# The first loads of a decoder-layer kernel: per-channel vectors ahead on ScalarE's DMA queue, the first 128 channels in two token halves, the other loads in SyncE's queue

## The chip, the cores and the metric

One core of one Trainium2 chip. The metric is the device time of one execution in microseconds (us). Lower is better.

## The reference, cut to what matters

One layer of a decoder trunk on 512 tokens with 1024 channels, all in float32:

```
h  = rmsnorm(x, g_mix)                       # gain g_mix per channel, factor r per token
z  = h @ w_in                                # w_in is 1024 x 9728
A  = retention(z...)                         # 4 heads
Bt = dilated window attention(z...)          # 3 groups of 4 heads, q and k normed and rotated
x  = x + (sig(g_A) * (A @ w_ret_out) + sig(g_B) * (Bt @ w_att_out)) @ w_o
x  = x + relu(rmsnorm(x, g_mlp) @ w_up)^2 @ w_down
x  = x + sig(rmsnorm(x, g_ple) @ w_ple_gate) * (p @ w_ple_proj)
```

The change is at the very beginning: the loading of x and of the first columns of w_in, and the first product h @ w_in, for the queries of attention group 0. There x is multiplied by g_mix alone; the token factor r is put in later.

## The kernel before, in words

**Split products.** Every float32 operand is split into a high part that TensorE takes in its float32r form and the low rest. A product is three matmuls of 128 x 128 by 128 x 512: high by high (L243), high by low (L244), low by high (L245). ScalarE makes the high parts (for weights `whi`, L231; for x `hh`, L452), VectorE the low ones (`wlo`, L232; `hl`, L453).

**First loads (`setup`, L383).** x arrives transposed, as 8 blocks of 128 channels by 512 tokens (`xr`, 256 KB each, L393); the weights of the first product arrive as 8 blocks of 128 rows by 512 columns (`raw`, 256 KB each, L395). All go out on SyncE's queue (SP), x block and weight block in turn, but for two: the first weight block and `gcol` go out on ScalarE's queue (ACT), in that order. `gcol` (128 x 40, 20 KB, L397) holds the per-channel vectors, g_mix in its first 8 columns. Behind these come, all on SP, the rotation table (L431), gains (L435), the four x tiles of 128 tokens (512 KB each, L404) and the next weights (L194). Seven matmuls on zeros (L414) keep TensorE busy meanwhile.

**The first product (`first_panel`, L444).** For each channel block k, ScalarE writes `hh` = x times gain (L452) and VectorE `hl` = x times gain minus `hh` (L453), each in one instruction over 512 tokens. The weight block is split at L231 and L232; for block 0 alone VectorE makes `whi` with a copy (L227) instead. TensorE takes block 0 in a written order: high by high for token tiles 0 to 3 (L471), then `hl` by `whi` for the four (L473), then `hh` by `wlo` (L475). Blocks 1 to 3 follow for the four token tiles, then blocks 4 to 7 tile by tile. Each finished tile is handed to `consume` (L590): four squares with sums on ScalarE (L595), then a rotation on VectorE (L548 to L553). Ahead of the first of these, ScalarE takes the squares of the four x tiles (`token_squares`, L515, L521), whose sums are used for r.

**Order.** In this stretch ScalarE and VectorE take their instructions in the order in which they are written (`manual_schedule`, `keep_in_program_order`); TensorE's order is the scheduler's. The second product (keys) begins where the first ends; its weights are split at L231 and L232 within the queue of the rotations: the first two units behind token tile 1, the others behind tile 3 and the next tables (L577). It uses the same four accumulators, each free when its rotation has read it.

Of the kernel before, what the change touches and what calls it, by code (L numbers as in the profile page):

```python
# [13 lines left out]
AF = mybir.ActivationFunctionType  # L14
ALU = mybir.AluOpType
AX = mybir.AxisListType

P = 128
S = 512
# [52 lines left out]
def R(ap):  # L72
    return ap.bitcast(F32R)


class Block:
# [306 lines left out]
    def setup(self):  # L383
        nc, a = self.nc, self.a
        self.gcol = self.const.tile([P, 40], F32, name="gcol")
        xr = [self.big("xr") for _ in range(2)]
        self.x_cols = [xr[k // 4][:, k % 4] for k in range(KD)]
        for u in range(KD // 2):
            src, _ = self.plan[u]
            raw = self.wraw.tile([P, 1024], F32, tag="raw", name=self.nm("raw")).rearrange("p (k n) -> p k n", k=2)  # L390
            for k in range(2):
                c = slice((2 * u + k) * P, (2 * u + k + 1) * P)
                nc.sync.dma_start(self.x_cols[2 * u + k], a["x_cols"][c])  # L393
                queue = nc.sync if u or k else nc.scalar
                queue.dma_start(raw[:, k], src[k * P : (k + 1) * P])  # L395
                if queue is nc.scalar:
                    nc.scalar.dma_start(self.gcol, a["vec_cols"])  # L397
            self.raws.append((raw, None))
        self.load_tables()
        self.x_tiles = []  # L400
        xb = [self.big("x") for _ in range(2)]
        for t in range(NT):
            v = xb[t // 2].rearrange("p (t c) n -> p t (c n)", t=2)[:, t % 2]
            nc.sync.dma_start(v, a["x"][0, t * P : (t + 1) * P])  # L404
            self.x_tiles.append(v)
        self.fetch(6)
        self.ident = self.const.tile([P, P], F32, name="ident")
        make_identity(nc, self.ident)
        warm = self.tmp("warm")
        nc.vector.memset(warm, 0.0)  # L410
        nc.scalar.activation(warm[:, 500:501], warm[:, 501:502], AF.Copy)
        wb, wps = warm.bitcast(mybir.dt.bfloat16), self.bank("warm")
        for _ in range(WARM):
            nc.tensor.matmul(wps, wb[:, :P], wb[:, :512], start=True, stop=True)  # L414
        self.mhalf = self.const.tile([P, H], F32, name="mhalf")
        nc.gpsimd.memset(self.mhalf, -0.5)
# [27 lines left out]
    def first_panel(self, consume, tables):  # L444
        nc = self.nc
        self.hT = self.new_act(2, "h")
        us = []

        def split_x(k):
            g = self.gcol[:, k : k + 1]  # L450
            h, l = (part[k // 4][:, k % 4] for part in self.hT)
            self.pin(nc.scalar.activation(R(h), self.x_cols[k], AF.Copy, scale=g))  # L452
            nc.vector.scalar_tensor_tensor(R(l), self.x_cols[k], g, h, op0=ALU.mult, op1=ALU.subtract)  # L453

        self.pinned = True
        for u in range(KD // 2):
            self.hook = lambda i: split_x(2 * u + i)
            us += self.units(1)
        self.hook = None
        self.pinned = False  # L460
        banks = [self.gbank() for _ in range(NT)]

        def part(t, k):
            wh, wl = us[k // 2]
            sh, sl = self.stat(self.hT, k, t, False)
            self.mm3(banks[t], sh, sl, wh[:, k % 2], wl[:, k % 2], k == 0, k == KD - 1)

        (wh, wl), mm = us[0], nc.tensor.matmul
        parts = [self.stat(self.hT, 0, t, False) for t in range(NT)]
        for t, (sh, _) in enumerate(parts):  # L470
            mm(banks[t], sh, wh[:, 0], start=True, stop=False)  # L471
        for t, (_, sl) in enumerate(parts):
            mm(banks[t], sl, wh[:, 0], start=False, stop=False)  # L473
        for t, (sh, _) in enumerate(parts):
            mm(banks[t], sh, wl[:, 0], start=False, stop=False)  # L475
        for k in range(1, KD // 2):
            for t in range(NT):
                part(t, k)
        tables()
        self.token_squares()  # L480
        for t in range(NT):
            for k in range(KD // 2, KD):
                part(t, k)
            consume(t, banks[t])
            if t == 1:
                self.pinned = True
                self.ahead(2)
                self.pinned = False
            self.tick()
# [83 lines left out]
    def tables(self, g, n):  # L573
        C = self.tabp.tile([P, NT, HD], F32, tag="tab", name=self.nm("C"))
        Sn = self.tabp.tile([P, NT, HD], F32, tag="tab", name=self.nm("S"))
        for o, part, gi in ((C, 0, 2 * n), (Sn, 1, 2 * n + 1)):
            ins = self.nc.vector.tensor_tensor(  # L577
                o, self.rc[:, 0, :, part * HD : (part + 1) * HD],
                self.gains[:, g, gi].unsqueeze(1).to_broadcast([P, NT, HD]), op=ALU.mult)
            if g == 0:  # L580
                self.tc.keep_in_program_order(ins)
        return C, Sn
# [615 lines left out]
```

## Time and profile before

| | |
|---|---|
| median of 3 runs | 1002.8 us (1002.75 to 1003.02) |
| the profiled execution's own time | 1002.82 us |
| its span in the profile | 1001.1 us |
| TensorE (PE) busy | 991.2 us, 99% of the span |
| VectorE (DVE) busy | 639.5 us, 64% |
| ScalarE (ACT) busy | 445.3 us, 44% |
| first real matmul starts | 6.38 us into the span |

The profiled execution took 1.7 us more than its span. PE's matmuls are pipelined, so that the step between two starts says more than the time of one. PEld is TensorE's weight load. SPq and ACTq are the sequencers of SyncE and ScalarE, where DMAs are issued. An arrow, "<-", names what ended the idle time.

### The profile page before, as it was taken

Reading aid. Unit: us, or ns where it says so; the run is one execution under the profiler, and the core shown is the slowest. Engines: PE = TensorE matmul, PEld = TensorE weight load, DVE = VectorE, ACT = ScalarE, POOL = GpSimd, SP = SyncE. Lnnn points to the kernel's source line nnn. Section 1 sums busy time; section 2 is a strip of 40 time slices with the busy share of each in tenths; the row PEclk is TensorE's granted clock in tenths of the full one; section 3 lists DMA queues with packets and bytes.
Section 4 is the critical chain, followed back from the end, with each engine's and each line's share of the span. In section 5 each row is a group of like instructions: output and inputs, shape, how many; then the busy total and the mean of one; then the engine's idle time right before and its main releaser. Section 6 shows DMA issues by size and latency. Waiting matters only on the chain.

```text
span 1001.1 us, 12319 instructions
## 1 busy us (share of the span) xinstructions
PE 991.2 (99%) x4604; PEld 827.9 (83%) x4604; DVE 639.5 (64%) x931; ACT 445.3 (44%) x844; POOL 98.1 (10%) x98
## 2 busy tenths in 40 slices
PE   8999999999999999999999999999999999999998
PEld 6888899889887888888888877888888888888886
DVE  5967675764779345554643698568468558656953
ACT  6435344433534325342422445654454356355451
POOL 0210220220000010001002010101101001010000
PEclk9999999999999999999999999999999999999999
DMA  9622122323254412222446486849749856784911
GB/s 349 240 84 77 53 84 84 105 86 105 71 159 121 123 43 84 85 82 87 134 142 165 128 211 189 209 110 235 196 112 214 229 146 161 218 183 115 310 54 53
DMA packets 89756, 141.14 MB, mean 141 GB/s; under 512 B 6320, under 2 KB 38368, under 8 KB 89696
## 3 DMA queue, kind: packets, MB, share of 16 engines
q1 hardware_dynamic: 78528, 119.09, 36.7%
q0 software_dynamic: 10880, 20.97, 12.5%
q8 instruction: 36, 0.59, 0.2%
q10 hardware_dynamic: 288, 0.28, 0.1%
q14 instruction: 24, 0.20, 0.1%
HBM read 136.09 MB, written 4.24 MB: 140 GB/s over the span
## 4 chain that ended last, share of the span: by engine, by line
PE 96%; DVE 2%; issue 1%; DMA 0%; ACT 0%; ACTq 0%; DVEq 0%
PE pg L245 27%; PE pg L243 27%; PE pg L244 27%; PE pb L243 2%; PE pb L245 2%; PE pb L244 2%; PE po L692 1%; PE ph L563 1%; DVE wlo L232 1%; PE sc L669 1%; PE pt L319 1%; PE ry L872 1%; PE pe L643 1%; DVE x L993 1%; PE kv L860 1%
## 5 line engine op out<-in xcount | busy, mean ns | idle before, releaser
L232 DVE TENSOR_TENSOR wlo<-raw,whi 128x1024 fp32r<-128x1024 f32 (+1 forms) x198 | 235.2, 1194 | 115.3 <-ACT whi L231 113.3
L231 ACT ACTIVATE whi<-raw 128x1024 fp32r<-128x1024 f32 (+1 forms) x197 | 202.5, 1036 | 207.4 <-PE pg L245 84.9
L243 PE MATMUL pg<-whi,hh 128*128 128x512 f32 x476 | 196.6, 414 | 0.0
L245 PE MATMUL pg<-whi,hl 128*128 128x512 f32 x476 | 186.7, 392 | 0.0
L244 PE MATMUL pg<-wlo,hh 128*128 128x512 f32 x476 | 186.3, 391 | 0.0
L245 PEld LDWEIGHTS pg<-whi,hl 128*128 128x128 f32 x476 | 97.1, 204 | 16.7
L244 PEld LDWEIGHTS pg<-wlo,hh 128*128 128x128 f32 x476 | 97.6, 205 | 13.8
L243 PEld LDWEIGHTS pg<-whi,hh 128*128 128x128 f32 x476 | 97.4, 205 | 14.1 <-DVE v L147 0.3
L245 PE MATMUL pg<-h2h,wlo 128*128 128x512 f32 x256 | 99.5, 389 | 0.4 <-DVE wlo L232 0.4
L243 PE MATMUL pg<-h2h,whi 128*128 128x512 f32 x256 | 99.6, 389 | 0.0
L244 PE MATMUL pg<-h2l,whi 128*128 128x512 f32 x256 | 99.6, 389 | 0.0
L196 POOL DMA_DIRECT2D raw<-in_w_down x32 | 38.6, 1206 | 305.9 <-DMA raw<-in_w_down 197.9
L244 PE MATMUL pg<-wlo,uh 128*128 128x512 f32 x160 | 62.4, 390 | 0.5 <-DVE wlo L232 0.5
L243 PE MATMUL pg<-whi,uh 128*128 128x512 f32 x160 | 62.7, 393 | 0.0
L245 PE MATMUL pg<-whi,ul 128*128 128x512 f32 x160 | 62.5, 392 | 0.0
L245 PEld LDWEIGHTS pg<-h2h,wlo 128*128 128x128 f32 x256 | 48.1, 188 | 10.9 <-DVE wlo L232 0.8
L244 PEld LDWEIGHTS pg<-h2l,whi 128*128 128x128 f32 x256 | 48.1, 188 | 10.0
L243 PEld LDWEIGHTS pg<-h2h,whi 128*128 128x128 f32 x256 | 48.1, 188 | 9.9
L243 PE MATMUL pg<-hh,whi 128*128 128x512 f32 x128 | 52.4, 409 | 0.0
L966 DVE TENSOR_TENSOR ul<-z,uh 128x1792 fp32r<-128x1792 f32 x20 | 40.5, 2025 | 15.5 <-ACT uh L965 15.5
L245 PE MATMUL pg<-hh,wlo 128*128 128x512 f32 x128 | 50.0, 390 | 0.0
L244 PE MATMUL pg<-hl,whi 128*128 128x512 f32 x128 | 49.9, 390 | 0.0
(203 smaller groups left out, 1629.2 us busy)
## 6 DMA issues: line engine op xcount, KB each, us to landing
raw<-in_w_in SPq DMA_DIRECT2D x72, 512.0 KB, 3.9
raw<-in_w_down SPq DMA_DIRECT2D x48, 512.0 KB, 4.6
raw<-in_w_up SPq DMA_DIRECT2D x32, 512.0 KB, 5.0
raw<-in_w_down POOLq DMA_DIRECT2D x32, 512.0 KB, 6.3
raw<-in_w_o SPq DMA_DIRECT2D x12, 512.0 KB, 3.6
x<-in_x SPq DMA_DIRECT2D x8, 512.0 KB, 6.3
raw<-in_w_ret_out SPq DMA_DIRECT2D x8, 512.0 KB, 3.5
raw<-in_w_o POOLq DMA_DIRECT2D x8, 512.0 KB, 5.8
```

What stands on the lines that cost most here:

```text
L196: self.nc.gpsimd.dma_start(raw, rows(add[0]), accum_op=ALU.add)
L231: self.pin(nc.scalar.activation(R(hi[:, i]), raw[:, i], AF.Copy))
L232: nc.vector.tensor_tensor(R(lo[:, i]), raw[:, i], hi[:, i], op=ALU.subtract)
L243: t.matmul(ps, sh, mh, start=first, stop=False, skip_group_check=more)
L244: t.matmul(ps, sh, ml, start=False, stop=False, skip_group_check=more)
L245: t.matmul(ps, sl, mh, start=False, stop=last, skip_group_check=more)
L319: nc.tensor.transpose(ps[:, k * P : (k + 1) * P], part[:, k * P : (k + 1) * P], self.ident)
L563: self.nc.tensor.transpose(ps[:, t * P : (t + 1) * P], rots[t][:, h * HD : (h + 1) * HD], self.ident)
L643: self.nc.tensor.transpose(ps[:, k * P : (k + 1) * P], e[:, k * P : (k + 1) * P], self.ident)
L669: nc.tensor.matmul(sc[:, h * P : (h + 1) * P], qT[:, h, rs], kT[:, h, rs], start=True, stop=True)
L692: nc.tensor.matmul(po[:, h * P : (h + 1) * P], v[:, vt, h * HD : (h + 1) * HD], pt, start=b == 0, stop=b == len(blocks) - 1)
L966: nc.vector.tensor_tensor(R(lo), src, hi, op=ALU.subtract)
```

## The change

The load of `gcol` becomes the first and only load on ScalarE's queue. The first weight block moves to SyncE's queue. The first x block is loaded in two halves of 256 tokens, one ahead of the first weight block and one behind it. For channel block 0, `hh` and `hl` are made in two instructions of 256 tokens each. Nothing else is edited.

```diff
+        nc.scalar.dma_start(self.gcol, a["vec_cols"])
         for u in range(KD // 2):
             src, _ = self.plan[u]
             raw = self.wraw.tile([P, 1024], F32, tag="raw", name=self.nm("raw")).rearrange("p (k n) -> p k n", k=2)
             for k in range(2):
                 c = slice((2 * u + k) * P, (2 * u + k + 1) * P)
-                nc.sync.dma_start(self.x_cols[2 * u + k], a["x_cols"][c])
-                queue = nc.sync if u or k else nc.scalar
-                queue.dma_start(raw[:, k], src[k * P : (k + 1) * P])
-                if queue is nc.scalar:
-                    nc.scalar.dma_start(self.gcol, a["vec_cols"])
+                x = lambda i: nc.sync.dma_start(self.x_cols[2 * u + k][:, i], a["x_cols"][c, i])
+                first = u == 0 and k == 0
+                x(slice(0, 256) if first else slice(0, S))
+                nc.sync.dma_start(raw[:, k], src[k * P : (k + 1) * P])
+                if first:
+                    x(slice(256, S))
             self.raws.append((raw, None))
...
         def split_x(k):
             g = self.gcol[:, k : k + 1]
             h, l = (part[k // 4][:, k % 4] for part in self.hT)
-            self.pin(nc.scalar.activation(R(h), self.x_cols[k], AF.Copy, scale=g))
-            nc.vector.scalar_tensor_tensor(R(l), self.x_cols[k], g, h, op0=ALU.mult, op1=ALU.subtract)
+            for c in (slice(0, 256), slice(256, S)) if k == 0 else (slice(0, S),):
+                self.pin(nc.scalar.activation(R(h[:, c]), self.x_cols[k][:, c], AF.Copy, scale=g))
+                nc.vector.scalar_tensor_tensor(R(l[:, c]), self.x_cols[k][:, c], g, h[:, c], op0=ALU.mult, op1=ALU.subtract)
```

## Rows read from the trace of the kernel before

**Rows 1.** The profile page's shares of busy time, and who waited for whom on PE over the whole span (us in total, times, longest).

```profile
PE 991.2 (99%) x4604; PEld 827.9 (83%) x4604; DVE 639.5 (64%) x931; ACT 445.3 (44%) x844; POOL 98.1 (10%) x98
PE pg L471 <- ACT hh L452: 1.8, 1, 1.8
PE warm L414 <- DVE warm L410: 1.5, 1, 1.5
PE pg L244 <- DVE wlo L232: 0.5, 1, 0.5
PE pt L319 <- DVE y L366: 0.4, 1, 0.4
PE pg L245 <- DVE wlo L232: 0.4, 1, 0.4
PE ph L563 <- DVE ro L553: 0.3, 1, 0.3
```

**Rows 2.** The chain that ended last, its pieces from 0.7 to 11.4 us (start, length, what).

```profile
0.74 0.41 ACTq L395
1.17 4.35 DMA gcol<-in_vec_cols
5.61 0.73 ACT hh L452
6.38 2.07 PE pg L471 x4
8.46 1.71 PE pg L473 x4
10.16 0.95 PE pg L475 x4
11.12 0.23 PE pg L243
```

**Rows 3.** The timeline from 0 to 5 us: the first issues, the zeros' matmuls and the copy of the first weight block (start, length, engine, line, what).

```profile
0.74 0.85 SPq L393 DMA_DIRECT2D xr<-in_x_cols  x2
1.46 3.17 PE L414 MATMUL warm<-warm 128*128 128x512 bf16 x7 [1.46 <-DVE warm L410]
1.65 0.42 SPq L395 DMA_DIRECT2D raw<-in_w_in  x1
4.71 0.43 DVE L227 CAST whi<-raw 128x512 fp32r<-128x512 f32 x1 [3.31 <-DMA raw<-in_w_in]
```

**Rows 4.** DMA issues in narrow stretches of the first 2 us: KB each and us from issue to landing. The first two were issued at 0.74, the third at 1.17 and the last at 1.65 us.

```profile
xr<-in_x_cols SPq DMA_DIRECT2D x1, 256.0 KB, 3.8
raw<-in_w_in ACTq DMA_DIRECT2D x1, 256.0 KB, 4.0
gcol<-in_vec_cols ACTq DMA_DIRECT2D x1, 20.0 KB, 4.3
raw<-in_w_in SPq DMA_DIRECT2D x1, 256.0 KB, 4.4
```

**Rows 5.** Busy time by stretches (PE, PEld, DVE, ACT, POOL with counts, then PE's granted clock, the DMA engines' share and GB/s).

```profile
1.60:2.00 0.40, 0.40 (x2) 0.14 (x1) 0.00 (x0) 0.35 (x1) 0.00 (x0) 1.00 0.67 97
2.00:2.40 0.40, 0.40 (x3) 0.12 (x2) 0.00 (x0) 0.40 (x1) 0.00 (x0) 1.00 0.47 87
2.40:2.80 0.40, 0.40 (x3) 0.12 (x2) 0.00 (x0) 0.40 (x1) 0.00 (x0) 1.00 0.60 148
8.00:10.00 2.00, 2.00 (x7) 1.51 (x6) 2.00 (x4) 1.82 (x5) 0.00 (x0) 1.00 1.02 376
14.00:20.00 6.00, 6.00 (x28) 4.99 (x27) 3.87 (x7) 3.00 (x5) 0.00 (x0) 1.00 1.05 398
```

**Rows 6.** Durations of the same kind of instruction at 128 and at 512 columns (ns min/median/max), of all that read gcol.

```profile
L327 ACT ACTIVATE A<-pt,gcol x32: 348/367/368, 378.2 to 448.0; 128x128 fp32r<-128x128 f32 x32
L328 DVE SCALAR_TENSOR_TENSOR A<-pt,gcol,A x32: 340/350/353, 378.6 to 448.4; 128x128 fp32r<-128x128 f32 x32
L452 ACT ACTIVATE hh<-xr,gcol x8: 704/722/726, 5.6 to 14.0; 128x512 fp32r<-128x512 f32 x8
L453 DVE SCALAR_TENSOR_TENSOR hl<-xr,gcol,hh x8: 746/747/751, 6.4 to 15.2; 128x512 fp32r<-128x512 f32 x8
```

**Rows 7.** The timeline of ACT from 18 to 24 us: the squares of the x tiles and the first token tile's.

```profile
18.11 1.06 ACT L521 ACTIVATE j<-x 128x1024 f32<-128x1024 f32 x1 [2.82 <-DMA x<-in_x]
19.45 1.06 ACT L521 ACTIVATE j<-x 128x1024 f32<-128x1024 f32 x1 [0.19 <-DMA x<-in_x]
22.01 1.06 ACT L521 ACTIVATE j<-x 128x1024 f32<-128x1024 f32 x1
23.07 0.26 ACT L595 ACTIVATE j<-pg 128x128 f32<-128x128 f32 x1
23.97 0.22 ACT L595 ACTIVATION_READ_ACCUMULATOR j<-pg 128x1 f32 x1
```

**Rows 8.** The timeline of DVE from 24 to 41 us, its rows around the weight splits of the second product.

```profile
24.22 0.69 DVE L548 TENSOR_TENSOR ro<-pg,C 128x512 f32<-128x512 f32 x1 [6.04 <-ACT j L595]
28.88 0.68 DVE L610 TENSOR_TENSOR ro<-ro,r 128x512 f32<-128x512 f32 x1
29.48 2.49 DVE L232 TENSOR_TENSOR wlo<-raw,whi 128x512 fp32r<-128x512 f32 x4
32.49 0.74 DVE L551 TENSOR_TENSOR ro<-pg,S 128x256 f32<-128x256 f32 x2
38.31 0.69 DVE L610 TENSOR_TENSOR ro<-ro,r 128x512 f32<-128x512 f32 x1 [0.90 <-POOL r L601]
40.13 4.62 DVE L232 TENSOR_TENSOR wlo<-raw,whi 128x1024 fp32r<-128x1024 f32 x4
```

**Rows 9.** The timeline of PE where the second product begins and where its second half of channels begins.

```profile
30.02 0.61 PE L243 MATMUL pg<-whi,hh 128*128 128x512 f32 x2
30.47 0.39 PE L244 MATMUL pg<-wlo,hh 128*128 128x512 f32 x1
40.90 0.84 PE L243 MATMUL pg<-whi,hh 128*128 128x512 f32 x3
41.58 0.39 PE L244 MATMUL pg<-wlo,hh 128*128 128x512 f32 x1
```

## The prediction, made before the changed kernel was run

> **What bounds the kernel now.** I read the page's busy shares first, then PE's waits: PE is busy 99% of the span, and of its idle time 1.8 us, the largest piece, lies in one place, the first real matmul waiting for `hh` [rows 1]. The others together are 1.6 us, plus 1.5 us before the zeros' matmuls. So a change at the start pays only by what it moves PE, and only as far as PE then stays ahead of nothing else.
>
> The chain of waits says what that first matmul stood behind [rows 2]: ScalarE's sequencer issues the weight block (0.41 us), then `gcol` at 1.17; `gcol` lands 4.35 us later at 5.52; `hh` takes 0.73 us; PE starts at 6.38. The weight block itself landed earlier: VectorE's copy of it ran from 4.71 to 5.14 [rows 3]. So `gcol`, 20 KB, was 0.8 us later than 512 KB of data.
>
> The reader should see one more thing in the chain: the first 8 matmuls step by 0.427 us (1.71 us for four), 512 columns at 1.2 GHz, though the granted clock reads 1.00 there [rows 2, 5]; from 11.12 on the step is 0.227, which is 2.4 GHz. PE had run zeros from 1.46 to 4.63 [rows 3], idled 1.75 us, and rose some 3.6 us after it restarted.
>
> **The change, part by part.**
>
> *`gcol` first on ScalarE's queue.* Its issue moves from 1.17 to 0.74, 0.43 us sooner. With its old latency of 4.35 it lands at 5.09; if it lands like the x block issued at 0.74 (3.8 us [rows 4]), at 4.54. It no longer stands behind a 256 KB block in its queue, so I take 4.6.
>
> *First half of the x block.* Issued at 0.74 as before, with half the bytes: no later than 4.54 [rows 4].
>
> *`hh` and `hl` in halves.* A 128x256 ScalarE instruction lies between 367 ns at 128 columns and 722 at 512: 0.485 us on a line through both; VectorE's between 350 and 747: 0.48 [rows 6]. Two of each cost 0.25 and 0.22 us more than one whole, on engines that are idle here. First half of `hh` ready: 4.6 + 0.09 + 0.485 = 5.2.
>
> *The weight block on SP.* It goes behind the x half; SP issues two in 0.85 us [rows 3], so its issue moves from 0.74 to 1.17: later, not sooner. Landing from below: by its end 20 + 128 + 256 = 404 KB have moved against 512 KB before, 108 KB less, and at 376 GB/s [rows 5] that is 0.29 us before 4.71, so 4.4. From above: 1.17 plus 4.2, between the first two and the fourth latency [rows 4], is 5.4. I take 4.9, the middle. The copy (0.43) ends at 5.33 and PE starts about 5.4. The binding load is then the weight block, no longer `gcol`. Against 6.38 that is 1.0 us sooner; bounds 0.5 (landing at 5.4) and 1.2 (`hh` at 5.2).
>
> The Trainium skill ("DMA: Bandwidth & Descriptors", section "Issuing engines are not separate DMA queues") says that issuing from several engines saves only the sequencer's issue time. By it the weight block would lose just its 0.43 us of issue, landing at 5.14 and starting PE at 5.6, 0.8 us sooner; that is inside my bounds.
>
> *Second x half.* Third on SP, at about 1.65. The load issued there before took 4.4 us [rows 4], for twice the bytes: 6.05 at worst, 4.8 if only the bytes ahead count. `hh`'s second half follows in 0.49 us, so 5.3 to 6.5; PE wants it after two matmuls at 0.427, at 6.25. Most likely no wait, at worst 0.25 us.
>
> *The clock.* If the clock rises at the same instant as before, a start 1.0 us sooner puts 1.0/0.427 = 2.3 more matmuls into the slow stretch, worth 2.3 x 0.227 = 0.5 us. If it rises as long after the start as before, the gain is 1.0. If the shorter idle (0.8 instead of 1.75 us) lets it rise at once, the 12 matmuls of block 0 take 2.7 us instead of 4.7: gain 3.0. I take 0.5 to 1.0.
>
> *What is late next.* This decides. PE's work to 30 us becomes earlier by 0.5 to 1.0, but what follows needs VectorE. Follow it backwards. The second product's first `wlo` is made from 29.48, four in 2.49 us, the first ending at 30.10 [rows 8]; PE's first use is at 30.47 [rows 9]: 0.37 us of slack. Its second half of channels needs the `wlo` made from 40.13, done about 1.2 us later at 41.3; PE's first use is at 41.58: slack 0.25. From 24.22 to there VectorE idles in one place only, 0.90 us for POOL's power of its own last result [rows 8], so this chain has a start and no play. Its start at 24.22 waited for ScalarE's squares of token tile 0, ending 24.19, and these began at 23.07, right behind the squares of the x tiles, which began as each tile landed: 18.1, 19.4, 22.0 [rows 7]. The x tiles are at the end of a stream that runs at 376 to 398 GB/s [rows 5]. Its bytes are unchanged. So VectorE's chain stays put, and PE, arriving 0.5 to 1.0 us sooner, waits for `wlo` at L244. Of the gain, 0.25 us is left.
>
> *The stream's own shift.* Until 2.8 us the DMA engines were half idle and moved (97 + 87 + 148) x 0.4 = 133 KB [rows 5]. If the number of packets is what is fixed there, halving or shrinking them costs up to half, 67 KB or 0.18 us; if not, nothing. From below, one queue in place of two could also gain, but no row shows idle engines after 2.8 us, so at most 0.1. I take 0.05 later. One more DMA on SP is another 0.43 us of issue, hidden: blocks land 0.67 us apart at that rate.
>
> Sum: 0.25 - 0.05 = 0.2 us less, on the profiled execution's 1002.82 (span 1001.1 and 1.7 around it), which is the median of 1002.8 within 0.02: **1002.6 us**. Own range of this case: 1002.3 to 1002.9. A measurement of this kernel can tell about 0.2%, 2.0 us, from no change; this is a tenth of it.
>
> **Rivals.**
>
> *The shift is kept (chance 0.22).* The scheduler already lets PE take one L243 more ahead of the first L244 at 30 us, and two at 41 [rows 9]; each further one adds 0.23 us of slack, and TensorE's order is not written by hand. With two or three more the whole 0.5 to 1.0 is kept: 1001.8 to 1002.3. Against it: nothing in the diff touches that place. With the clock up at once it could be more, but there is a stop: token tile 2's accumulator is read until 32.49 + 0.74 = 33.2 [rows 8], and PE wants it 24 matmuls after 30.02, at 35.5. So at most 2.2 us: 1000.6. I give the part above 2.0 us 0.03.
>
> *The x tiles come later, and all behind them (chance 0.13).* Place: the squares at L521. Small packets and one more transfer make the stream later by d; VectorE's chain moves by d, and from d = 0.25 us on PE pays all of it. With d = 0.18 plus a second 0.43 us, should the extra issue not be hidden, d = 0.6 and the time is 1002.82 + 0.35 = 1003.2. For it: 160-byte and 1 KB rows. Against: SP issues faster than blocks land. The Trainium skill ("DMA: Bandwidth & Descriptors", section "Rules for kernel authors") speaks against the split: coalesce small transfers into large ones. No row here shows two half loads beside one whole.
>
> *PE does not start sooner (chance 0.10).* If the weight block on SP lands after 5.8, or `gcol`'s small packets still finish at 5.5 beside the x half, PE starts at about 6.1 to 6.4 and nothing moves: 1002.8.
>
> **How the numbers follow.** Forecast 0.55, kept 0.22, later x tiles 0.13, no earlier start 0.10. Faster by over 0.2%: 0.03 from the kept shift with an early clock, and 0.01 for what I don't see; slower by over 0.2%: d would have to be 2.3 us, 0.02; within 0.2%: 0.94. The range takes the forecast, the third rival, the kept shift up to 1.2 us and most of the second: 1001.6 to 1003.2.
>
> **What would show it.** Right: `gcol` out of the chain, VectorE's copy in its place, PE's first real matmul at 4.9 to 5.9, the fourth x tile's squares still at 22.0, VectorE's rotation still at 24.2, and new PE waits on `wlo` at about 30 or 41 us whose sum eats most of the earlier start. Wrong: a PE timeline that is still 0.5 us or more ahead at 45 us, or squares of the x tiles that moved by over 0.3 us. A first matmul later than 6.1 would refute the first step.

## The result, and the profile after

The changed kernel takes 1005.48 us, the median of 10 runs (1004.24 to 1010.79), beside 1003.13 us for the kernel before (10 runs, 1002.75 to 1004.38). The ratio is 1.0028, with a 95% interval of 1.002 to 1.0036: slower by 0.2 to 0.36%. The forecast was 1002.6 with a range of 1001.6 to 1003.2, so it was wrong in sign. The profiled execution of the changed kernel took 1004.24 us at a span of 1002.5, the fastest of its ten; that of before took 1002.82.

Lines moved by 3 in the code: L474 is the old L471, L524 the old L521, L598 the old L595, L551 the old L548. First the start of the changed kernel: its timeline to 7 us, and the landing of what was issued from 0.5 to 2.7 us (KB each, us from issue to landing).

```profile
0.74 0.41 ACTq L388 DMA_DIRECT2D gcol<-in_vec_cols  x1
...
4.07 0.43 DVE L227 CAST whi<-raw 128x512 fp32r<-128x512 f32 x1 [2.66 <-DMA raw<-in_w_in]
...
4.64 1.92 PE L474 MATMUL pg<-whi,hh 128*128 128x512 f32 x4
...
6.40 1.09 PE L476 MATMUL pg<-whi,hl 128*128 128x512 f32 x4
```

```profile
raw<-in_w_in SPq DMA_DIRECT2D x2, 256.0 KB, 4.0
xr<-in_x_cols SPq DMA_DIRECT2D x2, 128.0 KB, 2.7
xr<-in_x_cols SPq DMA_DIRECT2D x1, 256.0 KB, 4.2
gcol<-in_vec_cols ACTq DMA_DIRECT2D x1, 20.0 KB, 2.6
```

`gcol` lands 2.6 us after its issue, at 3.3, in place of 5.52 [rows 2]. VectorE's copy starts at 4.07 (4.71 before [rows 3]), PE at 4.64 (6.38) with no idle time behind the zeros, which end at 4.63 [rows 3], and from 6.40 on four matmuls take 1.09 us, the higher clock. Before, the same view has it at 9.96:

```profile
8.26 1.91 PE L473 MATMUL pg<-whi,hl 128*128 128x512 f32 x4
...
9.96 1.15 PE L475 MATMUL pg<-wlo,hh 128*128 128x512 f32 x4
```

The start did better than forecast.

Then what VectorE's chain hangs on: ScalarE's and VectorE's timelines from 18 to 43 us, and PE's where the second product begins.

```profile
19.64 1.06 ACT L524 ACTIVATE j<-x 128x1024 f32<-128x1024 f32 x1 [2.80 <-DMA x<-in_x]
...
23.55 1.06 ACT L524 ACTIVATE j<-x 128x1024 f32<-128x1024 f32 x1
...
24.61 0.26 ACT L598 ACTIVATE j<-pg 128x128 f32<-128x128 f32 x1
```

```profile
25.76 0.69 DVE L551 TENSOR_TENSOR ro<-pg,C 128x512 f32<-128x512 f32 x1 [6.03 <-ACT j L598]
...
31.02 2.49 DVE L232 TENSOR_TENSOR wlo<-raw,whi 128x512 fp32r<-128x512 f32 x4
...
41.66 2.35 DVE L232 TENSOR_TENSOR wlo<-raw,whi 128x1024 fp32r<-128x1024 f32 x2
```

```profile
29.79 0.47 PE L243 MATMUL pg<-whi,hh 128*128 128x512 f32 x1 [1.38 <-DVE ro L554]
31.76 0.50 PE L244 MATMUL pg<-wlo,hh 128*128 128x512 f32 x1 [1.50 <-DVE wlo L232]
...
43.03 0.40 PE L244 MATMUL pg<-wlo,hh 128*128 128x512 f32 x1
```

Read them against [rows 7 to 9]. The first x tile's squares came 1.53 us later (18.11 before), the rotation 1.54 (24.22), the two stretches of `wlo` 1.54 and 1.53 (29.48, 40.13), and PE's L244 1.45 (41.58). The execution became 1.42 us longer. PE's earlier start ended as 2.9 us of waiting. The waits of PE say the same (compare [rows 1]):

```profile
PE pg L244 <- DVE wlo L232: 2.2, 3, 1.5
...
PE pg L243 <- DVE ro L554: 1.4, 1, 1.4
```

The chain of work that ended last now runs through the loads (pieces from 3.5 to 26 us; before it went through `gcol` and PE [rows 2]):

```profile
3.54 5.86 DMA raw<-in_w_in
...
9.41 5.39 DMA raw<-in_w_in
...
14.82 8.65 DMA x<-in_x
...
23.55 1.15 ACT j L524 x2
24.70 1.04 ACT j L598 x8
...
25.76 0.69 DVE ro L551
```

So the stream was late. Its rate stands last in the rows of busy time by stretches, behind the DMA engines' share: four rows of before, then the changed kernel's.

```profile
2.00:8.00 6.00, 4.25 (x11) 1.95 (x10) 2.06 (x4) 3.53 (x7) 0.00 (x0) 1.00 0.96 338
4.00:6.00 2.00, 0.63 (x2) 0.00 (x0) 0.43 (x1) 0.39 (x1) 0.00 (x0) 1.00 1.05 373
4.00:5.20 1.20, 0.63 (x2) 0.00 (x0) 0.43 (x1) 0.00 (x0) 0.00 (x0) 1.00 1.05 373
5.20:8.00 2.80, 1.61 (x4) 1.33 (x5) 1.64 (x3) 2.39 (x5) 0.00 (x0) 1.00 1.01 371
```

```profile
2.00:8.00 6.00, 5.99 (x18) 3.41 (x17) 2.66 (x5) 2.72 (x6) 0.00 (x0) 1.00 0.90 266
2.00:4.00 2.00, 2.00 (x7) 0.62 (x5) 0.00 (x0) 1.17 (x3) 0.00 (x0) 1.00 0.99 277
4.00:6.00 2.00, 1.99 (x5) 1.17 (x4) 1.66 (x4) 0.51 (x1) 0.00 (x0) 1.00 0.78 213
8.00:10.00 2.00, 1.78 (x7) 0.96 (x6) 1.45 (x2) 1.62 (x3) 0.00 (x0) 1.00 0.97 346
3.60:4.00 0.40, 0.40 (x3) 0.12 (x1) 0.00 (x0) 0.26 (x1) 0.00 (x0) 1.00 1.19 215
4.40:4.80 0.40, 0.39 (x2) 0.19 (x2) 0.40 (x2) 0.18 (x1) 0.00 (x0) 1.00 0.60 128
4.00:5.20 1.20, 1.19 (x3) 0.50 (x2) 0.86 (x3) 0.51 (x1) 0.00 (x0) 1.00 0.63 175
5.20:8.00 2.80, 2.80 (x11) 2.29 (x10) 1.80 (x3) 1.04 (x2) 0.00 (x0) 1.00 0.96 298
```

From 2 to 8 us it is short by 72 GB/s x 6 us = 432 thousand bytes, from 8 to 10 us by 30 x 2 = 60 (376 before [rows 5]); at 388 GB/s, the changed kernel's rate from 14 to 20 us, these 492 are 1.27 of the 1.53 us. The loss has two parts. From 4.0 to 5.2 us, 238 thousand bytes are missing, and the engines' share is 0.63 in place of 1.05: they stood idle in part. From 5.2 to 8.0 us, 204 thousand are missing at a share of 0.96 in place of 1.01: there they were nearly as busy as before and moved a fifth less.

Another 1.2 us lie between the profiled execution (1004.24) and the median (1005.48). They go with TensorE's clock: its mean was 1.000 in that execution and 0.994 to 0.998 in the other nine, which took 1005.06 to 1010.79. A second profile shows where (`after_again`).

### The profile page after: what moved, and what is told of

The parts are those of the page before. It is cut to its first block, busy times and chain, and to the rows that moved or that the text cites. A ratio compares the mean times of both kernels' runs of the same rounds, so it can differ in the third digit from the quotient of the medians.

```text
span 1002.5 us, 12323 instructions
## 1 busy us (share of the span) xinstructions
PE 991.4 (99%) x4604; PEld 827.0 (83%) x4604; DVE 640.4 (64%) x932; ACT 446.4 (45%) x845; POOL 98.1 (10%) x98
## 4 chain that ended last, share of the span: by engine, by line
PE 93%; DVE 3%; DMA 2%; issue 1%; ACT 1%; SPq 0%; DVEq 0%; ACTq 0%
PE pg L245 26%; PE pg L244 26%; PE pg L243 26%; PE pb L244 2%; PE pb L245 2%; PE pb L243 2%; PE po L695 1%; PE ph L566 1%; DMA raw<-in_w_in 1%; DVE wlo L232 1%; DMA x<-in_x 1%; PE sc L672 1%; PE pt L319 1%; PE ry L875 1%; PE pe L646 1%
## 5 line engine op out<-in xcount | busy, mean ns | idle before, releaser
L244 PE MATMUL pg<-wlo,hh 128*128 128x512 f32 x476 | 186.6, 392 | 1.7 <-DVE wlo L232 1.7
L245 PE MATMUL pg<-whi,hl 128*128 128x512 f32 x476 | 186.7, 392 | 0.0
L244 PEld LDWEIGHTS pg<-wlo,hh 128*128 128x128 f32 x476 | 97.6, 205 | 16.2 <-DVE wlo L232 2.5
L245 PEld LDWEIGHTS pg<-whi,hl 128*128 128x128 f32 x476 | 97.1, 204 | 16.6
L245 PE MATMUL pg<-h2h,wlo 128*128 128x512 f32 x256 | 99.5, 389 | 0.4 <-DVE wlo L232 0.4
L244 PE MATMUL pg<-h2l,whi 128*128 128x512 f32 x256 | 99.6, 389 | 0.0
L244 PE MATMUL pg<-wlo,uh 128*128 128x512 f32 x160 | 62.4, 390 | 0.4 <-DVE wlo L232 0.4
L245 PE MATMUL pg<-whi,ul 128*128 128x512 f32 x160 | 62.5, 392 | 0.0
L245 PEld LDWEIGHTS pg<-h2h,wlo 128*128 128x128 f32 x256 | 48.1, 188 | 10.7 <-DVE wlo L232 0.9
L244 PEld LDWEIGHTS pg<-h2l,whi 128*128 128x128 f32 x256 | 48.1, 188 | 10.0
L245 PE MATMUL pg<-hh,wlo 128*128 128x512 f32 x128 | 50.0, 390 | 0.0
L244 PE MATMUL pg<-hl,whi 128*128 128x512 f32 x128 | 49.9, 390 | 0.0
```

Source lines behind the costliest of these rows:

```text
L244: t.matmul(ps, sh, ml, start=False, stop=False, skip_group_check=more)
L245: t.matmul(ps, sl, mh, start=False, stop=last, skip_group_check=more)
```

## The experiments

All runs are beside runs of the kernel before on the same chip (medians 1003.08 to 1003.41). "Squares" is where ScalarE's squares of the first x tile start. The first theory (Q): all first blocks in one queue thin the stream, two queues at work fill it. Rivals: the halves do it (H); `gcol`'s early issue does it (G); the early work of PE and ScalarE does it (E); later also the bytes that stand issued early (S). The stream's figures in each row are those of one profile. Two profiles of the same kernel differ by 0.2 to 1.1 us in the squares (e1 18.82 and 18.58, the changed kernel 19.64 and 20.76), so smaller differences between two rows are not to be relied on.

### What the stream's lag is worth: `e4_x_tiles_early`

The changed kernel with the x tiles issued ahead of the tables.

```diff
-        self.load_tables()
         self.x_tiles = []
...
+        self.load_tables()
```

> The kernel after with one edit: the four x tiles are loaded ahead of the rotation table and the gains. 768 KB at 390 GB/s are 2.0 us, so the x tiles' squares begin at 17.7 instead of 19.64 us. If VectorE's chain behind these squares carries the loss to the end, its rotation begins some 1.5 to 2 us sooner than 25.76 (then tables or PE's own tile hold it), PE's waits on it at 28 to 32 us (2.9 us) shrink below 1.5, and the time falls to 1001.5 to 1003, below both kernels at best. If something else carries the loss, the time stays at 1004 to 1006.

1002.84 us (1002.71 to 1005.51), ratio 1.0001 (0.9992 to 1.0011): 2.6 us less than the changed kernel. The stream is as thin (271 GB/s from 2 to 8 us, 210 from 4 to 6), but the squares start at 17.33 and the rotation at 24.63, now behind VectorE's table work, which waited for the gains. The wait of 1.4 us for the rotation is gone; that of 1.5 us for `wlo` remains. The same edit to the kernel before (`b4`, below) gains 0.04%, where this one gains 0.27%. So the loss does go through the x tiles.

### Which part thins it: five ways of issuing

`e1_one_queue` (and `e1_again`): the changed kernel without halves, `hh` and `hl` whole.

```diff
-                x(slice(0, 256) if first else slice(0, S))
+                nc.sync.dma_start(self.x_cols[2 * u + k], a["x_cols"][c])
                 nc.sync.dma_start(raw[:, k], src[k * P : (k + 1) * P])
-                if first:
-                    x(slice(256, S))
```

> The kernel after without its halves: gcol alone on ScalarE's queue, the first weight block on SP behind the whole first x block. Theory Q (one queue in place of two for the first blocks makes the stream slow from 4 to 9 us): the stream is as slow as after, the first x tile's squares near 19.6 us against 18.1 before, time 1004 to 1006. Theory H (the 1 KB rows of the half blocks make it slow): squares at 18.1 to 18.3, time 1002.4 to 1003.0. Theory G (gcol's early issue does): as Q.

> The changed kernel without the halves, all first blocks whole in SyncE's queue, run again. If one queue thins the stream also without halves: 310 to 325 GB/s from 2 to 8 us (338 before), squares at 18.4 to 19 us, 1003.3 to 1004.3 us. If its first profile was out of line: 335 GB/s or more, squares at 18.0 to 18.2 us, 1002.5 to 1003.1 us.

`e2_halves_two_queues`: the changed kernel with the first weight block on ScalarE's queue behind `gcol`.

```diff
-                nc.sync.dma_start(raw[:, k], src[k * P : (k + 1) * P])
+                (nc.scalar if first else nc.sync).dma_start(raw[:, k], src[k * P : (k + 1) * P])
```

> The kernel after, but the first weight block stays on ScalarE's queue, behind gcol. Theory Q: the stream is that of before, squares at 18.1 to 18.3 us, time 1002.4 to 1003.0. Theory H: squares near 19.6, time 1004 to 1006. Theory G: as H.

`e3_gcol_first`: the kernel before with `gcol` issued ahead of the first weight block on the same queue, nothing else.

```diff
+        nc.scalar.dma_start(self.gcol, a["vec_cols"])
...
-                if queue is nc.scalar:
-                    nc.scalar.dma_start(self.gcol, a["vec_cols"])
```

> The kernel before with one edit: gcol ahead of the first weight block on ScalarE's queue. Theories Q and H: squares of the first x tile at 18.1 to 18.3 us, first real matmul at 5.3 to 5.6 instead of 6.38, time 1002.4 to 1003.0, since VectorE's chain stays put. Theory G: squares near 19.6, time 1004 to 1006.

`g1_second_x_on_act`: the changed kernel with x block 1 on ScalarE's queue.

```diff
-                x = lambda i: nc.sync.dma_start(self.x_cols[2 * u + k][:, i], a["x_cols"][c, i])
+                queue = nc.scalar if u == 0 and k == 1 else nc.sync
+                x = lambda i: queue.dma_start(self.x_cols[2 * u + k][:, i], a["x_cols"][c, i])
```

> The kernel after with one edit: the second x block goes out on ScalarE's queue behind gcol, so that two queues carry first blocks while the first weight block stays second on SP. Theory Q (two queues keep the stream fast): 376 GB/s and more from 4 to 9 us, the x tiles' squares at 18.1 to 18.6 us instead of 19.64, PE starts at 4.6 to 5.2, time 1002.5 to 1003.5. Theory E (the stream is slow because the engines begin to work at 3.4 to 4.6 us, beside it): 210 to 310 GB/s from 4 to 8 us, squares near 19.5, time 1004 to 1006.

`h1_halves_adjacent`: the changed kernel with both halves ahead of the weight block.

```diff
+                if first:
+                    x(slice(256, S))
                 nc.sync.dma_start(raw[:, k], src[k * P : (k + 1) * P])
-                if first:
-                    x(slice(256, S))
```

> The changed kernel with the two halves of the first x block behind each other and the first weight block behind both, all in SyncE's queue; gcol alone on ScalarE's. If it is the two 1 KB-row halves in a single busy queue that thin the stream, whatever their order: GB/s of 4 to 6 us at 190 to 230, the first x tile's squares at 19.2 to 19.8 us, 1004 to 1005.5 us. If it is the whole weight block between the halves: 4 to 6 us at 310 or more, squares at 18.2 to 18.9 us, 1003 to 1004 us.

| | first blocks in | us (median) | ratio, 95% | GB/s 2 to 8 us | GB/s 4 to 6 us | squares |
|---|---|---|---|---|---|---|
| `e3` | two queues, whole | 1002.78 | 0.9995 (0.9986 to 1.0004) | 352 | 385 | 18.09 |
| `e2` | two, halves | 1002.94 | 0.9999 (0.9989 to 1.0008) | 348 | 383 | 18.63 |
| `g1` | two, halves | 1003.29 | 1.0002 (0.9992 to 1.0011) | 335 | 384 | 18.00 |
| `e1` | one, whole | 1003.87 | 1.0005 (0.9996 to 1.0015) | 318 | 314 | 18.82 |
| `e1_again` | one, whole | 1004.86 | 1.0013 (1.0004 to 1.0023) | 328 | 341 | 18.58 |
| `h1` | one, halves adjacent | 1004.35 | 1.0014 (1.0004 to 1.0023) | 295 | 320 | 19.08 |
| changed kernel | one, halves | 1005.48 | 1.0028 (1.002 to 1.0036) | 266 | 213 | 19.64 |

`gcol` first is not to blame, nor are halves as such: with two queues either keeps 383 to 385 GB/s from 4 to 6 us and the time of before, though e2's squares, at 18.63, are later than before and than Q had said. One queue alone costs something (e1's first interval takes in no change, its second does not), one queue with halves most. In all of these profiles the rotation starts 6.09 to 6.17 us after the squares (6.11 before, 6.12 in the changed kernel): VectorE's chain hangs on the x tiles whatever else moves. e1_again's rate fell between the two cases set for it and its time above both, and e3's PE started at 5.75, later than was said. h1 fell between its two cases: its rate from 4 to 6 us is that of the one, its squares are late as in neither, and it is thin earlier.

### Is it the engines' early work: `g2_gcol_late`

The changed kernel with `gcol` behind the second weight block on SP, so that PE and ScalarE begin late.

```diff
-        nc.scalar.dma_start(self.gcol, a["vec_cols"])
...
+                if u == 0 and k == 1:
+                    nc.sync.dma_start(self.gcol, a["vec_cols"])
```

> The kernel after with one edit: gcol goes out on SP behind the second weight block, so that one queue carries all and ScalarE, VectorE (but for the copy) and PE begin only at about 5.5 to 6.5 us. Theory Q: the stream is as slow as after (210 to 310 GB/s from 4 to 8 us), the x tiles' squares near 19.5. Theory E: the stream is that of before, squares at 18.1 to 18.6. Either way PE is less far ahead at 28 us, so that its stall there is under 2.5 us; time 1003.5 to 1005 by Q, 1002.6 to 1003.2 by E.

1004.75 us (1003.61 to 1005.12), ratio 1.0014 (1.0004 to 1.0023). PE starts at 8.16, yet the stream runs at 261 GB/s from 2 to 8 us and 196 from 4 to 6, and the squares start at 19.52. E falls. PE is ahead of nothing here and has no new wait; the 1.66 us that the median lost to that of before (1003.09) are about the 1.78 by which PE starts later. The mean clock stays at 0.998 to 1.000.

### One queue, or too few bytes: `i1`, `i2`, `j1`, `j2`

One queue and halves have something in common: an issue takes SP some 0.47 us, whether it carries 128 or 256 KB. Up to 2.2 us the kernel before issued 1280 KB in two queues (five blocks), e2 and g1 1024 KB, e1 1024 KB, the changed kernel and h1 768 KB, of which the last 256 only at 2.11 (`gcol`'s 20 KB not counted). That is S, and the next kernels set it against Q.

`i1_one_queue_pairs`: all in SP's queue, halves kept, the other blocks in pairs of 512 KB (`w2(0)` is weight blocks 0 and 1, `x2(1, 2)` x blocks 1 and 2).

```diff
+        nc.sync.dma_start(self.x_cols[0][:, 0:256], a["x_cols"][0:P, 0:256])
+        w2(0)
+        nc.sync.dma_start(self.x_cols[0][:, 256:S], a["x_cols"][0:P, 256:S])
+        x2(1, 2)
+        w2(1)
+        x2(3, 1)
...
```

> The changed kernel with all first blocks still in SyncE's queue and the halves kept, but the others loaded in pairs (512 KB in one DMA where two blocks lie side by side): first half, weight blocks 0 and 1, second half, x blocks 1 and 2, weight blocks 2 and 3, x block 3, then pairs. By 2.1 us some 1280 KB are issued in place of 768. If the stream is thin because too few bytes stand issued early (a 0.47 us issue for a half carries 128 KB): 330 GB/s or more from 2 to 8 us, the first x tile's squares at 18.0 to 18.5 us. If one queue by itself feeds the DMA engines thinly: 260 to 320 GB/s, squares at 18.8 us or later. PE starts later in either, since its first weight block lands with the second.

`i2_late_block_on_act`: the changed kernel with weight block 1 on ScalarE's queue, written behind its table load (`late` is that block's pair of operands, taken out of SP's loop).

```diff
         nc.scalar.activation(warm[:, 500:501], warm[:, 501:502], AF.Copy)
+        nc.scalar.dma_start(*late)
```

> The changed kernel with the second weight block issued on ScalarE's queue behind its table load, at about 2.7 us, where SyncE issued it at 2.6: the same bytes issued at nearly the same times, but two queues at work from about 3.7 us on. If a second queue at work is what fills the stream: 330 GB/s or more from 4 to 6 us in place of 213, squares at 18.0 to 18.8 us, 1003 us. If it is the bytes that stand issued early: 200 to 250 GB/s from 4 to 6 us, squares at 19.2 us or later, 1004 us or more.

`j1_two_queues_quarters`: e3 with the first x block in four DMAs of 32 partitions.

```diff
-                nc.sync.dma_start(self.x_cols[2 * u + k], a["x_cols"][c])
+                for p in range(0, P, P if u or k else P // 4):
+                    q = slice(p, p + (P if u or k else P // 4))
+                    nc.sync.dma_start(self.x_cols[2 * u + k][q], a["x_cols"][c][q])
```

> The kernel before with gcol first on ScalarE's queue and the first x block loaded in four quarters of 32 partitions by SyncE (64 KB each, rows of 2 KB as before): two queues at work, whose issues up to 2.2 us carry 512 KB in place of 1280. If it is the bytes that stand issued early: 4 to 6 us at 300 GB/s or less (385 with the block whole), squares of the first x tile at 18.8 us or later, 1003.3 us or more. If two queues at work fill the stream by themselves: 360 to 390 GB/s, squares at 18.0 to 18.5 us, 1002.5 to 1003.2 us.

`j2_one_queue_partition_halves`: e1 with the first x block in two DMAs of 64 partitions around the first weight block.

```diff
-                nc.sync.dma_start(self.x_cols[2 * u + k], a["x_cols"][c])
+                halves = [slice(0, P)] if u or k else [slice(0, P // 2), slice(P // 2, P)]
+                nc.sync.dma_start(self.x_cols[2 * u + k][halves[0]], a["x_cols"][c][halves[0]])
                 nc.sync.dma_start(raw[:, k], src[k * P : (k + 1) * P])
+                for q in halves[1:]:
+                    nc.sync.dma_start(self.x_cols[2 * u + k][q], a["x_cols"][c][q])
```

> All first blocks in SyncE's queue, the first x block in two halves of 64 partitions around the first weight block, so that its rows stay 2 KB long and the packets as many as in the kernel before; hh and hl whole. If the halves hurt by taking an issue for half the bytes: 260 to 295 GB/s from 2 to 8 us, squares at 19.1 to 19.8 us, 1004 to 1005.5 us. If it is their 1 KB rows: as with whole blocks in one queue, 318 to 328 GB/s, squares at 18.5 to 18.9 us, 1003.8 to 1004.9 us.

| | queues, KB issued by 2.2 us | us (median) | ratio, 95% | GB/s 2 to 8 us | GB/s 4 to 6 us | squares |
|---|---|---|---|---|---|---|
| `i1` | one, 1280 | 1002.86 | 0.9996 (0.9986 to 1.0005) | 333 | 391 | 18.15 |
| `i2` | two, 1024 | 1002.94 | 0.9993 (0.9983 to 1.0002) | 339 | 378 | 18.16 |
| `j1` | two, 512 | 1005.57 | 1.0016 (1.0006 to 1.0025) | 267 | 237 | 19.46 |
| `j2` | one, 512 | 1004.32 | 1.0018 (1.0007 to 1.0029) | 282 | 222 | 19.47 |

The stretches of i1 (4 to 6 us) and of j1 (1.6 to 4.8 us), and j1's issues on SP:

```profile
4.00:6.00 2.00, 0.69 (x3) 0.10 (x1) 0.64 (x2) 0.29 (x1) 0.00 (x0) 1.00 1.03 391
```

```profile
1.60:2.00 0.40, 0.40 (x2) 0.14 (x1) 0.00 (x0) 0.33 (x1) 0.00 (x0) 1.00 0.59 92
2.00:4.00 2.00, 2.00 (x7) 0.62 (x5) 0.00 (x0) 1.16 (x2) 0.00 (x0) 1.00 0.94 241
4.00:4.40 0.40, 0.40 (x2) 0.00 (x0) 0.00 (x0) 0.00 (x0) 0.00 (x0) 1.00 0.25 46
4.40:4.80 0.40, 0.23 (x1) 0.00 (x0) 0.00 (x1) 0.00 (x0) 0.00 (x0) 1.00 0.66 159
```

```profile
0.74 2.25 SPq L396 DMA_DIRECT2D xr<-in_x_cols  x5
...
3.05 0.47 SPq L398 DMA_DIRECT2D raw<-in_w_in  x1
```

Q, as the number of queues by itself, falls twice: i1 fills the stream from one queue, j1 starves it with two. j1 shows how. Its four quarters, the first weight block and `gcol` are 532 KB (545 thousand bytes); by 4.0 us 92 x 0.4 + 241 x 2 = 519 thousand had moved (none before 1.6 us), and then the engines stood three quarters idle until x block 1, the fifth issue of that row, flowed. j2 keeps rows of 2 KB and thins the stream all the same, so the halves' short rows are not needed for it; but its issues on SP took 0.48 to 0.58 us each, longer than in the other runs, so that x block 1 went out at 2.50 us and not at 2.11. i2 did not do what it was made for: its issue on ScalarE started at 1.18 us, ahead of the table load, so more bytes stood issued early as well. It agrees with both S and Q.

S orders the runs only coarsely. At 1280 KB the rate from 4 to 6 us is 373 to 391 GB/s, at 512 to 768 KB it is 196 to 237 in five kernels; but h1 has 320 with 768 KB, the changed kernel's 213 is no more than j1's and j2's with 512, and 1024 KB give 314 and 341 in one queue, 378 to 384 in two. What is shown is that, with the other loads in blocks of 256 KB, one queue and halves together thin the stream, and that neither alone does so to this extent. That too few bytes stood issued is shown for j1's gap at 4.0 us; for the changed kernel it is an argument.

### The clock: `after_again`

The changed kernel unchanged, for a second profile.

> The changed kernel as it is, once more, for a second profile. If PE's stall at 28 to 32 us lets the clock fall in most executions: granted clock at 0.5 in a stretch from about 30 us on, mean clock 0.994 to 0.998, 1005 us or more; in an execution without the fall about 1004.2 us. The first x tile's squares at 19.4 to 19.9 us in either.

1005.68 us (8 runs, 1003.67 to 1007.72), ratio 1.0021 (1.001 to 1.0031). The profiled execution was the longest, 1007.72 us. Its stretches from 28 to 38 us (the last three columns are the granted clock, the DMA share and GB/s), and three rows of PE's timeline:

```profile
28.00:30.00 2.00, 0.67 (x2) 0.19 (x1) 1.90 (x6) 2.00 (x6) 0.77 (x1) 1.00 1.08 372
30.00:32.00 2.00, 0.50 (x1) 0.19 (x1) 1.97 (x6) 1.74 (x14) 1.51 (x3) 0.81 1.04 383
...
34.00:38.00 4.00, 4.00 (x11) 3.13 (x10) 3.97 (x10) 0.54 (x1) 1.06 (x1) 0.50 0.19 41
```

```profile
32.91 0.79 PE L244 MATMUL pg<-wlo,hh 128*128 128x512 f32 x1 [1.47 <-DVE wlo L232]
33.50 0.63 PE L245 MATMUL pg<-whi,hl 128*128 128x512 f32 x1
...
37.77 0.53 PE L244 MATMUL pg<-wlo,hh 128*128 128x512 f32 x1
```

PE was busy for 1.17 of the 4 us from 28 to 32, waiting for the late rotation and `wlo`; then the clock stood at 0.50, 1.2 GHz, until about 38 us. From 32.91 to 37.77 it did 11 steps in 4.86 us, which take 11 x 0.227 = 2.50 at 2.4 GHz: 2.36 us lost. The squares, at 20.76, were 2.65 us later than before (19.4 to 19.9 had been expected), and `wlo`, at 32.17, 2.69. 2.69 + 2.36 = 5.05, against 1007.72 - 1002.82 = 4.90 measured. The two of the eight runs with a mean clock of 0.999 or more took 1003.67 and 1004.71 us.

### A version that beats both: `f1`, with `f2` and `b4`

`f1_gcol_first_x_tiles` (and `f1_again`): the kernel before, with `gcol` first on ScalarE's queue and the x tiles ahead of the tables. `f2_halves_x_tiles`: e2 with the x tiles ahead. `b4_x_tiles_early`: the kernel before with the x tiles ahead only.

```diff
+        nc.scalar.dma_start(self.gcol, a["vec_cols"])
...
-                if queue is nc.scalar:
-                    nc.scalar.dma_start(self.gcol, a["vec_cols"])
             self.raws.append((raw, None))
-        self.load_tables()
         self.x_tiles = []
...
+        self.load_tables()
```

> The kernel before with two edits: gcol ahead of the first weight block on ScalarE's queue, and the four x tiles loaded ahead of the rotation table and gains. The x tiles' squares begin at 16.1 us instead of 18.1; the tables then wait for the gains, which land at about 22.0, so VectorE's rotation begins at 23.3 instead of 24.2 and PE keeps its 0.6 us: 1002.2 (1001.9 to 1002.6), below both kernels. If VectorE's chain is not the bound, no more than the 1002.8 of gcol first alone.

> The kernel before with gcol first on ScalarE's queue and the x tiles ahead of the tables, run again in more rounds. If its gain is real: 1001.4 to 1002.1 us, a ratio of 0.998 to 0.9993 that excludes 1. If it was chance: 1002.5 to 1003, a ratio that takes in 1.

> As the run before this one, with the first x block in halves as well (first weight block on ScalarE's queue behind gcol). PE starts at 5.35 instead of 5.75; rotation at 23.3. PE keeps 0.8 to 1.0 us: 1001.9 (1001.6 to 1002.5). If VectorE's chain is not the bound: 1002.9 as with the halves alone.

> The kernel before with nothing but the x tiles loaded ahead of the rotation table and the gains. If its start anchors VectorE's chain: the first x tile's squares at 15.2 to 15.7 us, the rotation at 22.8 to 23.2 us, and as PE is not sooner at its start it keeps only what it waits for now: 1002.3 to 1002.8 us. If the gain of the kernel with gcol first and x tiles early came from the x tiles alone: 1001.5 to 1002 us.

| | us (median, range) | ratio, 95% | PE starts | squares | rotation |
|---|---|---|---|---|---|
| `f1` | 1001.74 (1001.05 to 1002.77) | 0.9986 (0.9976 to 0.9995) | 5.63 | 15.47 | 22.78 |
| `f1_again` | 1002.17 (1000.98 to 1002.51) | 0.9987 (0.9978 to 0.9995) | 5.48 | 15.86 | 23.16 |
| `f2` | 1002.43 (1001.47 to 1003.64) | 0.9994 (0.9984 to 1.0003) | 5.38 | 15.81 | 23.12 |
| `b4` | 1002.98 (1001.75 to 1003.88) | 0.9996 (0.9987 to 1.0005) | 6.41 | 16.13 | 23.48 |

f1 is faster than the kernel before in both sets, by 0.13 to 0.14%. This fits the view that PE's earlier start needs the earlier VectorE chain, and the other way round: e3 moved PE's start alone to 5.75 and b4 the chain alone by 0.74, and neither differs from before by what its runs can tell. The intervals of f1, e3 and b4 overlap, so that f1's lead over these two is not shown. b4 missed its expectation: its squares came 0.4 us later than was said, and it gained less. f2's halves add nothing that its runs can tell.

## Why the prediction was wrong

**Right in kind, too small: the start.** `gcol` left the chain, and PE began earlier by 1.74 us where 1.0 was said, outside the bounds of 0.5 to 1.2. The copy ended at 4.50 in place of 5.33, even before the zeros: the term that was too large is the weight block's landing, 4.9 forecast. It landed 2.9 us after its issue at 1.18, at 4.04. In the second profile it landed 3.3 us after its issue, and PE began at 5.10 after 0.48 us of waiting for the copy, as the prediction has it.

**Too cautious: the clock.** 0.5 to 1.0 us was taken. Real matmuls followed the zeros almost at once, and the clock rose 1.76 us after the start. PE was 2.0 us ahead at 9.4 (L245 at 9.44, at 11.42 before).

**Right: what is late next.** VectorE's chain is anchored on the x tiles, and PE's gain ends in waits at about 30 us, 1.50 us of them on `wlo`; the other 1.38, for the rotation that frees the accumulator, were not named as a wait. All four links moved by 1.53 to 1.54 us together. With this shift as d, the rival's rule that PE pays d less 0.25 us gives 1002.82 + 1.28 = 1004.10; the profiled execution took 1004.24. (By the prediction's own rows the slack is nearer 0.3: 40.13 + 4.62 / 4 is 41.28, against 41.58.)

**Wrong: "the stream's own shift".** This is the step that failed, and with it "so VectorE's chain stays put". The shift was taken as 0.05 us, bounded by 0 and 0.18; it measured 1.53 and, in the second profile, 2.65. The bound came from the packets before 2.8 us, and the step said that one more DMA on SP is hidden since blocks land 0.67 us apart. That spacing is the full stream's. It left out that a load flows well after its issue: x block 1, issued at 2.11, landed at 6.3. Ahead of it stood 128 + 256 + 128 + 20 = 532 KB (545 thousand bytes), where the kernel before had issued 1044 KB by 1.65 us. From 1.6 to 4 us 64 x 0.4 + 277 x 2 = 580 thousand moved, these 545 and little more, and the rate fell to 128 GB/s at 4.4 to 4.8 us. That the one follows from the other is the likeliest reading, not a shown one. The rival "x tiles come later and all behind them" had the mechanism, with d = 0.6 at most; its price was too small by 0.9 us, and its chance with it.

**Not in the prediction at all: the clock can fall back.** The text priced a PE that waits at the length of the wait. After the stall from 28 to 32 us it may also restart at 1.2 GHz, which cost 2.4 us in the profile that shows it. Of both sets of runs the three with a mean clock of 0.999 or more took 1003.67, 1004.24 and 1004.71 us, 0.4 to 1.5 more than the median of before beside them, the other fifteen 1005.06 to 1010.79. So of the 2.35 us between the medians roughly half is the stream's lag itself and half the clock. This split is an estimate: the lag differs between executions, and a longer lag makes a longer stall.

The Trainium skill ("DMA: Bandwidth & Descriptors", section "Issuing engines are not separate DMA queues") says that issuing from several engines saves only the time of issue. i1 against j1 agrees: the number of queues does not decide by itself. e1 against e2 and g1 does not agree: with the same 1024 KB issued by 2.2 us, one queue gave 314 and 341 GB/s from 4 to 6 us, two gave 383 and 384. What the prediction drew from it was too little: it put the lost time of issue into the weight block's landing alone, and not into the loads behind it.

What stays open: why whole blocks in one queue (e1: 314 and 341 GB/s from 4 to 6 us) are slower than two queues with the same 1024 KB issued (e2, g1: 383, 384); why the changed kernel's stream stays below 350 GB/s until 10 us, although by 5.1 us it had issued 2304 KB, as many as the kernel before, and its engines were 96% busy from 5.2 to 8 us; and why h1, with the changed kernel's issued bytes, has 320 where that has 213.

## What to carry to other kernels

Count the bytes issued per microsecond of the issuing sequencer at the start, where nothing stands queued yet. Here a split load, together with a load moved behind others in the same queue, left the DMA engines partly without work some 2 us later; halves alone or one queue alone cost less (0 to 0.13%, against 0.28%). An earlier start of the bound engine was kept here where the chain behind the last loads moved with it: find that chain's anchor, and move both. Give an engine that will wait for microseconds a price for the clock as well as for the wait.

## What the runs showed of the hardware that was not expected

- In the changed kernel the 20 KB of `gcol`, alone on their queue, landed in 2.6 us, and the two halves of 128 KB in 2.7 in the median; the whole blocks issued at 2.11 and 2.59 us took 4.2 and 5.1.
- The clock's rise is not a function of the idle time alone: in j1 PE started at 6.26 after 1.63 us of idling and took its first four matmuls in 1.20 us, mostly at the higher clock; in e2 it started at 5.35 after only 0.73 us and took 3.55 us for the first eight, the lower clock.
- A stall of PE at about 27 to 33 us does not settle by its length whether the clock falls. After two waits of 2.88 us together the clock stayed at 1.00 in the changed kernel's first profile; it fell to 0.50 after 3.42 us in its second, after 2.91 in e1's and after 2.27 in e1_again's.
